# Up-projection of a gated ConvFFN: 28 of 44 pairs of tiles by seven half products in place of eight

## Chip, cores, metric

The kernel runs on one core of a Trainium2 chip. The metric is the device time of one execution in microseconds, the median of several runs; a profiled execution of the same program gives the trace.

## What is computed

Two layers of a hybrid encoder on 768 tokens (512 of one request, 256 of another), all in float32. Each layer has an adaLN norm, one input projection split into dilated window attention and a convolution group, an output projection, and then a gated ConvFFN. The change touches the ConvFFN:

```python
def conv_ffn(h, w_up, dw_w, w_down):
    a, g = jnp.split(h @ w_up, 2, axis=-1)
    g = depthwise_conv(g, dw_w)          # width 3 along the tokens, within each request
    return (a * jax.nn.gelu(g)) @ w_down
# D_MODEL = 1024, D_FF = 2816; in trunk, per layer:
#   h = rms_norm(x, norm2_g[l]) * (1 + s2) + sh2 ;  x = x + g2 * conv_ffn(h, ...)
```

## The kernel before

Activations lie with features on the 128 partitions and the 768 tokens along the free axis. A float32 product is made of three fast ones: every operand is kept as a rounded high part and the remainder, the low part (`hi`, `lo`), and `three` (L349) issues low weight times high activation, high times low, high times high into one PSUM bank. A weight tile is 128 x 1024 (eight slices of 128 x 128, one "unit"). `product` (L358) runs one unit against the eight activation tiles `h`, first the 512 tokens, then the 256: 24 matmuls of 512 columns and 24 of 256.

The 2816 hidden features make 22 pairs of tiles a layer, 44 in all: unit `a` and unit `g` of the up-projection. A pair is two calls of `product`; then `hidden` (L859) scales `g` on ScalarE, adds the two neighbours on VectorE, applies GELU on ScalarE, multiplies by `a` on VectorE, splits the result into `hh` (ScalarE) and `hl` (GpSimd). Pairs come in chunks of 4, 4, 4, 4, 2, 4 (`CHUNKS`). Behind the first pair of a chunk stands `part` (L448), the down-projection of the chunk before, with `nk` units of 48 matmuls each; its results are added to `x` by `accumulate` on VectorE. The last chunk runs its four pairs first, then the part, then `last_part`.

Weights come as a stream of tiles (`stream`, L183). `load_ahead` issues the load of a tile into one of five buffers `raw`; `consume` (L306) splits a tile: `hi` and the negative of the tile on ScalarE (`wh`, `wl`), and a DMA from GpSimd's queue that adds the raw tile to `wl`. Four pairs of `hi`/`lo` buffers (`PAIRS`) hold split units; `unit` pops one, `release` gives it back. In the FFN of layer 0, 56 tiles of the adaLN weights are mixed into the stream (`spread`, `ADA_FFN`); each takes two dot products on VectorE (`ada_dots`, L288).

The order of instructions on each engine is made by the Python program itself: it keeps a clock that the matmuls advance (`tick`), `feed` consumes the next stream item when enough of that clock has passed and buffers are free, and background generators (`conv_bg`) are stepped at a rate. Each engine then runs its own instructions in that order.

Of the kernel before, what the change touches and what calls it, by code (L numbers as in the profile page):

```python
# [15 lines left out]
ALU = mybir.AluOpType  # L16
# [22 lines left out]
ACT = 28  # L39
# [3 lines left out]
ADA_FFN = (2, 56)  # L43
# [13 lines left out]
def encoder(ctx: ExitStack, tc: tile.TileContext, xT, cT, rel_bias, onehot, nlog, wada, wadaT, wada_g2, bada,  # L57
# [19 lines left out]
    def wide(name, w):  # L77
        return act.tile([P, w], F32, tag="wide", name=name, bufs=5)
# [146 lines left out]
    raws = [it[1] if it[0] == "w" else wada[it[3] + KD * (it[2] == 2), it[4]] if it[0] == "a" else wada_g2[it[2] - 40] if it[1] == 0 else wadaT[it[1] - 1, it[2]] for it in stream]  # L225
    loaded = []
    state = {"item": 0, "live": 0, "n": 0, "fed": 0.0, "hold": True}
    ready = []

    def load_ahead(n):  # L230
        while len(loaded) < min(len(raws), n):
            r = wraw.tile([P, 8 * P], F32, tag="raw", name=f"raw{len(loaded)}")
            nc.sync.dma_start(r, raws[len(loaded)])
            loaded.append(r)

# [70 lines left out]
    def consume():  # L306
        i = state["item"]
        it = stream[i]
        state["item"] += 1
        load_ahead(i + RAW)  # L310
        r = loaded[i]
        state["fed"] = clock[0]
        if it[0] == "a":
            ada(*it[1:], r)
            return
        if it[0] == "d":
            ada_dots(*it[1:], r)
            return
        n = state["n"]
        state["n"] += 1  # L320
        state["live"] += 1
        hi = whl.tile([P, 8 * P], F32R, tag="hi", name=f"wh{n}")
        lo = whl.tile([P, 8 * P], F32R, tag="lo", name=f"wl{n}")
# [6 lines left out]
        ready.append((hi, lo))  # L330
# [525 lines left out]
    def ffn(l, K, hs, nxt):  # L856
# [16 lines left out]

        f = 0
        pend = []
        for n, nk in enumerate(CHUNKS):
            hold = nk if n == len(CHUNKS) - 1 else 1
            hid = []
            for i in range(nk):
                if f == 0:  # L880
                    us = [kslices(unit()) for _ in range(2)]
                    a, g = product(us, hs, f"u{l}_{f}", key)
                    release(2)
                else:
                    (a,) = product([kslices(unit())], hs, f"a{l}_{f}")
                    release()
                    (g,) = product([kslices(unit())], hs, f"g{l}_{f}")
                    release()
                hid.append(hidden(f, a, g))
# [28 lines left out]
    load_ahead(RAW)  # L918
# [138 lines left out]
```

## Time and profile before

| | |
|---|---|
| median of 3 runs | 1902.55 us (1900.71 to 1903.45) |
| profiled execution: device time, span | 1892.81 us, 1891.0 us |
| TensorE (PE) busy | 1840.4 us, 97% of the span |
| VectorE (DVE) busy | 1000.3 us, 53% |
| ScalarE (ACT) busy | 816.8 us, 43% |
| GpSimd (POOL) busy | 367.4 us, 19% |
| DMA | 261.81 MB, mean 138 GB/s |

Matmuls are pipelined and their ends are modelled, so the duration of one (0.39 us for 512 columns) is longer than the distance between the starts of two; rates are read from starts. The span is that of the profiled execution; the sums of the prediction are made against it.

### The profile page before, as it was taken

The page shows a single profiled execution, that of the slowest core. Times are in us where ns is not written, and L with a number is a line of the kernel's source. Part 1 is how long each engine was busy: PE and PEld are TensorE (multiplying, and loading weights), DVE is VectorE, ACT ScalarE, POOL GpSimd, SP SyncE. Part 2 cuts the span into 40 slices and gives each one's busy share as a digit, 9 for nine tenths or more (in the row PEclk, how much of TensorE's full clock was granted, in tenths as well). Part 3 has the DMA queues.
Part 4 walks back from the last instruction along what each step waited for, and adds up shares of the span by engine and source line. Part 5 has one row for each costly group of instructions (what it writes and reads, how often), then busy time and mean ns, then how long its engine had stood idle before and what let it go on. Part 6 is the DMA issues. An engine that isn't in the chain of part 4 may idle for free.

```text
span 1891.0 us, 27649 instructions
## 1 busy us (share of the span) xinstructions
PE 1840.4 (97%) x11164; PEld 1552.1 (82%) x11164; DVE 1000.3 (53%) x1779; ACT 816.8 (43%) x1315; POOL 367.4 (19%) x344
## 2 busy tenths in 40 slices
PE   6999999999999999999999999999899999999999
PEld 4789676778888888888878986768788888888888
DVE  6667666776655655664367886666622221313123
ACT  3324667554423242433343357675543333333331
POOL 1103110033211121211232131100521121211110
PEclk9999999999999999999999999999999999999999
DMA  9666431236667777685635542223457464646454
GB/s 339 176 174 192 122 90 44 67 90 162 184 191 199 212 183 212 156 228 147 145 86 127 124 119 64 65 59 97 93 131 162 106 148 112 149 100 151 101 122 112
DMA packets 80913, 261.81 MB, mean 138 GB/s; under 512 B 9137, under 2 KB 18609, under 8 KB 80785
## 3 DMA queue, kind: packets, MB, share of 16 engines
q0 software_dynamic: 26640, 97.01, 28.4%
q1 hardware_dynamic: 54144, 163.03, 25.4%
q8 instruction: 88, 1.44, 0.3%
q14 instruction: 41, 0.33, 0.1%
HBM read 159.83 MB, written 3.18 MB: 86 GB/s over the span
## 4 chain that ended last, share of the span: by engine, by line
PE 90%; DVE 3%; ACT 2%; issue 2%; DMA 2%; POOL 1%; SPq 0%; POOLq 0%; ACTq 0%; DVEq 0%
PE a L351 6%; PE g L351 6%; PE g L352 6%; PE a L352 6%; PE a L350 6%; PE g L350 6%; PE pd L351 5%; PE pd L352 5%; PE pd L350 5%; PE s L729 4%; PE tp L763 2%; PE o L774 2%; PE v L350 1%; DMA wl<-raw 1%; PE q L350 1%
## 5 line engine op out<-in xcount | busy, mean ns | idle before, releaser
L329 POOL DMA_DIRECT2D wl<-raw x185 | 163.9, 886 | 691.1 <-ACT wl L328 498.0
L324 ACT ACTIVATE wh<-raw 128x1024 fp32r<-128x1024 f32 x188 | 197.2, 1049 | 163.4 <-PE pd L352 69.1
L866 DVE SCALAR_TENSOR_TENSOR gc<-g,fw_sb,gc 128x511 f32<-128x511 f32 x84 | 51.4, 612 | 389.6 <-ACT gc L865 389.6
L558 DVE SCALAR_TENSOR_TENSOR acc<-up,cw_sb,acc 128x783 f32<-128x783 f32 x240 | 246.8, 1028 | 4.3
L328 ACT ACTIVATE wl<-raw 128x1024 fp32r<-128x1024 f32 x185 | 193.4, 1046 | 0.0
L351 PE MATMUL pd<-hl,wh 128*128 128x512 f32 (+1 forms) x576 | 193.2, 335 | 0.0
L352 PE MATMUL pd<-hh,wh 128*128 128x512 f32 (+1 forms) x576 | 192.8, 335 | 0.0
L350 PE MATMUL pd<-hh,wl 128*128 128x512 f32 (+1 forms) x576 | 192.4, 334 | 0.0
L871 POOL TENSOR_TENSOR hl<-gc,hh 128x768 fp32r<-128x768 f32 x44 | 81.8, 1860 | 543.5 <-ACT hh L870 543.5
L865 ACT ACTIVATE gc<-g,fw_sb 128x512 f32<-128x512 f32 x84 | 48.2, 573 | 305.6 <-PE g L352 305.6
L292 DVE CUSTOM_DVE_ANT_0 cro<-raw,cr 128x1024 f32<-128x1024 f32 x112 | 166.6, 1488 | 4.2 <-ACT cr L285 1.5
L445 DVE SCALAR_TENSOR_TENSOR x<-pd,mod,x 128x512 f32<-128x512 f32 (+1 forms) x160 | 96.3, 615 | 133.9 <-PE pd L352 133.9
L350 PEld LDWEIGHTS pd<-hh,wl 128*128 128x128 f32 x576 | 108.1, 188 | 12.3
L351 PEld LDWEIGHTS pd<-hl,wh 128*128 128x128 f32 x576 | 108.3, 188 | 11.7
L352 PEld LDWEIGHTS pd<-hh,wh 128*128 128x128 f32 x576 | 108.2, 188 | 11.4
L868 ACT ACTIVATE gc<-gc 128x512 f32<-128x512 f32 x88 | 46.2, 525 | 130.1 <-DVE gc L867 130.1
L729 PE MATMUL s<-kT,qT 64*128 64x512 f32 (+1 forms) x192 | 94.1, 570 | 0.0
L869 DVE TENSOR_TENSOR gc<-a,gc 128x512 f32<-128x512 f32 x84 | 46.9, 558 | 55.0 <-ACT gc L868 55.0
L741 ACT ACTIVATE sp<-sp,nm 128x512 f32<-128x512 f32 (+1 forms) x96 | 62.1, 647 | 27.5 <-DVE nm L739 24.6
L739 DVE CUSTOM_DVE_ANT_0 sp<-s,G 128x512 f32<-128x512 f32 (+1 forms) x96 | 57.1, 596 | 24.0 <-PE s L729 24.0
L750 ACT ACTIVATE sp<-sp,den 128x512 f32<-128x512 f32 (+1 forms) x96 | 61.8, 645 | 9.0 <-DVE den L748 8.8
L764 ACT ACTIVATE PT<-tp 128x512 f32<-128x512 f32 (+1 forms) x96 | 49.3, 518 | 22.5 <-PE tp L763 21.9
(697 smaller groups left out, 5165.2 us busy)
## 6 DMA issues: line engine op xcount, KB each, us to landing
wl<-raw POOLq DMA_DIRECT2D x185, 512.0 KB, 5.8
raw<-in_w_up SPq DMA_DIRECT2D x88, 512.0 KB, 4.7
raw<-in_wadaT SPq DMA_DIRECT2D x48, 512.0 KB, 5.7
raw<-in_w_down SPq DMA_DIRECT2D x44, 512.0 KB, 4.5
raw<-in_w_in SPq DMA_DIRECT2D x40, 512.0 KB, 4.7
raw<-in_wada SPq DMA_DIRECT2D x24, 512.0 KB, 7.0
raw<-in_w_out SPq DMA_DIRECT2D x16, 512.0 KB, 4.7
G<-bt SPq DMA_DIRECT2D x16, 448.0 KB, 4.5
```

The lines of the kernel that those rows point to most:

```text
L292: nc.vector.tensor_tensor_reduce(out=rows["out"], in0=r, in1=rows[g], op0=ALU.mult, op1=ALU.add, scale=1.0, scalar=0.0, accum_out=mod[l][: ...
L324: nc.scalar.activation(hi, r, AF.Copy)
L328: nc.scalar.activation(lo, r, AF.Copy, scale=-1.0)
L329: nc.gpsimd.dma_start(out=lo, in_=r, accum_op=ALU.add)
L350: nc.tensor.matmul(ps, wl, xh, start=first, stop=False)
L351: nc.tensor.matmul(ps, wh, xl, start=False, stop=False)
L352: nc.tensor.matmul(ps, wh, xh, start=False, stop=last)
L445: nc.vector.scalar_tensor_tensor(x[ot][:, span(g)], ps, mod[l][:, gate + ot, g:g + 1], x[ot][:, span(g)], op0=ALU.mult, op1=ALU.add)
L558: nc.vector.scalar_tensor_tensor(a, up[i][:, t:t + ACW], K["cw"][:, l, i, t:t + 1], a, op0=ALU.mult, op1=ALU.add)
L729: nc.tensor.matmul(ps[:, :w], qT[hp][64 * s:64 * s + 64, o + i * P:o + (i + 1) * P], kT[hp][64 * s:64 * s + 64, o:o + w], start=True, stop ...
L741: nc.scalar.activation(sp[:, :w], sp[:, :w], AF.Exp, scale=-1.0, bias=nm, accum_out=den)
L871: nc.gpsimd.tensor_tensor(lo, gc, hi.bitcast(F32), op=ALU.subtract)
```

## The change

In layer 0 the 10 pairs from chunk 3 on, in layer 1 the 18 pairs from chunk 1 on (`SEVEN = (3, 1)`), are computed by Strassen's scheme in the variant with 15 additions. The tokens are cut into two halves of 384 (`HALF`), the 1024 input features into two halves of four tiles, and the two outputs are `a` and `g`: a 2 x 2 product of blocks with seven block products, each of 4 x 3 matmuls of 384 columns (84 in a pair; before 96, of 512 and 256).

- **Weights.** The stream has for such a pair the items A (unit of `a`, split as before), G (the raw tile of `g`, kept), S, B, R. S, B and R make sums of blocks of the raw tiles and split them: sums and low parts on VectorE, high parts on ScalarE. All three are split units in the same four buffers; R overwrites the raw `g` tile.
- **Tokens.** `token_sums` makes 12 split blocks of 384 columns once a layer, as a background generator (`SUMS_FROM`, `SUMS_RATE`), and `last_sums` four more, in place of half of the tiles `h`, just before the first seven-product pair.
- **Products.** `seven(f)` uses three PSUM banks X, Y, Z: X takes the first product, is copied by ScalarE, and goes on accumulating; it is copied twice more. VectorE adds Y and Z to the copies; then convolution, GELU and multiplication as before, from SBUF.
- **The rest of the stream.** The adaLN tiles of layer 0 now lie between items 1 and 29 of the FFN (`ADA_FFN`; before 2 and 56); `token_sums` makes its last four blocks only when none of them is left in the stream. `ACT` grows from 28 to 29 buffers.

```diff
-ACT = 28
+ACT = 29
+HALF = NT // 2
+SEVEN = (3, 1)
+SUMS_FROM = (8, 1)
+SUMS_RATE = (0.7, 1.1)
-ADA_FFN = (2, 56)
+ADA_FFN = (1, 29)
...
+                    ff += [("A", ups[0]), ("G", ups[1]), ("S", None), ("B", None), ("R", None)]
...
+    def split(hi, lo, r):
+        nc.scalar.activation(hi, r, AF.Copy)
+        nc.vector.tensor_tensor(lo, r, hi.bitcast(F32), op=ALU.subtract)
+
+    def sums(n, r, hi, lo):
+        a, g = held["a"], held["g"]
+        s = held["s"] = wraw.tile([P, 8 * P], F32, tag="raw", name=f"sum{n}")
+        nc.vector.tensor_tensor(s[:, :512], g[:, :512], g[:, 512:], op=ALU.add)
+        nc.vector.tensor_tensor(s[:, 512:], s[:, :512], a[:, :512], op=ALU.subtract)
+        split(hi, lo, s)
+
+    def last_block(n, r, hi, lo):
+        split(hi[:, :512], lo[:, :512], held["g"][:, 512:])
+
+    def differences(n, r, hi, lo):
+        a, g, s = held["a"], held["g"], held["s"]
+        nc.vector.tensor_tensor(g[:, :512], a[:, :512], g[:, :512], op=ALU.subtract)
+        nc.vector.tensor_tensor(g[:, 512:], a[:, 512:], s[:, 512:], op=ALU.subtract)
+        split(hi, lo, g)
...
-            if stream[state["item"]][0] != "w" or len(ready) < 2 and state["live"] < PAIRS:
+            kind = stream[state["item"]][0]
+            if kind in "adG" or state["live"] < PAIRS and len(ready) < (2 if kind == "w" else 3):
                 consume()
...
+        def last_sums():
+            for k in range(4):
+                t, u = (tmp(f"{c}4{l}{k}", False)[:, :HALF] for c in "tu")
+                p, q, to = column(k + 4, 0), blocks[1, k], column(k, 1)
+                nc.vector.tensor_tensor(t, p[0].bitcast(F32), q[0].bitcast(F32), op=ALU.subtract)
+                nc.vector.tensor_tensor(u, p[1].bitcast(F32), q[1].bitcast(F32), op=ALU.subtract)
+                nc.vector.tensor_tensor(t, t, u, op=ALU.add)
+                nc.scalar.activation(to[0], t, AF.Copy)
+                nc.vector.tensor_tensor(to[1], t, to[0].bitcast(F32), op=ALU.subtract)
...
+        def seven(f):
...
+            add(X, ua, 0, b11, True)
+            av = af(f"av{tag}")
+            S.activation(av[:, left], X, AF.Copy)
+            add(Y, ua, 1, b21, True)
+            release()
+            V.tensor_tensor(av[:, left], Y, av[:, left], op=ALU.add)
+            us = unit()
+            add(X, us, 1, t2, False)
+            S.activation(av[:, right], X, AF.Copy)
+            add(Z, us, 0, t1, True)
+            release()
+            ub = unit()
+            ur = unit()
+            add(X, ur, 0, t3, False)
+            gv = af(f"gv{tag}")
+            S.activation(gv[:, left], X, AF.Copy)
+            V.tensor_tensor(gv[:, right], Z, gv[:, left], op=ALU.add)
+            add(Y, ub, 0, t4, True)
+            release()
+            V.tensor_tensor(gv[:, left], Y, gv[:, left], op=ALU.add)
+            add(Z, ur, 1, b22, False)
+            release()
+            V.tensor_tensor(av[:, right], Z, av[:, right], op=ALU.add)
...
+                S.activation(z, gv[:, o:o + w], AF.Copy, scale=w1)
+                V.scalar_tensor_tensor(z[:, 1:], gv[:, o:o + w - 1], w0, z[:, 1:], op0=ALU.mult, op1=ALU.add)
+                V.scalar_tensor_tensor(z[:, :w - 1], gv[:, o + 1:o + w], w2, z[:, :w - 1], op0=ALU.mult, op1=ALU.add)
+                S.activation(z, z, AF.Gelu_apprx_tanh)
+            for z, (o, w) in zip(zs, GROUPS):
+                V.tensor_tensor(av[:, o:o + w], av[:, o:o + w], z, op=ALU.mult)
+            hi, lo = at(f"hh{tag}"), at(f"hl{tag}")
+            S.activation(hi, av, AF.Copy)
+            nc.gpsimd.tensor_tensor(lo, av, hi.bitcast(F32), op=ALU.subtract)
...
+            if n == SEVEN[l]:
+                while conv_bg["gen"] is not None:
+                    conv_step(True)
+                last_sums()
             for i in range(nk):
-                if f == 0:
+                if f == SUMS_FROM[l]:
+                    conv_bg.update(gen=token_sums(), rate=SUMS_RATE[l], acc=0.0)
+                if n >= SEVEN[l]:
+                    hid.append(seven(f))
```

Three places in the order of the engines. First ScalarE in layer 1 around the end of pair 5. In the rows a name is tile, layer, pair: `g1_5` is the product g of layer 1, pair 5; `wh`/`wl` are split weights, `hh` the high part of the hidden tile. Before:

```order
L865 ACTIVATE gc1_5_13440<-g1_5_00_13383,fw_sb_265 128x512
L868 ACTIVATE gc1_5_13440<-gc1_5_13440 128x512
L865 ACTIVATE gc1_5_13440<-g1_5_01_13415,fw_sb_265 128x256
L868 ACTIVATE gc1_5_13440<-gc1_5_13440 128x256
L870 ACTIVATE hh1_5_13441<-gc1_5_13440 128x768
L324 ACTIVATE wh140_13461<-raw220_13204 128x1024
L328 ACTIVATE wl140_13462<-raw220_13204 128x1024
```

The change, same place (`gz` is the convolved gate, `wh165` the high part of R for pair 6, the next; `av1_6<-x1_6` the first copy out of bank X of pair 6; `wh166` the unit A of pair 7):

```order
L1053 ACTIVATE gz1_50_13781<-gz1_50_13781 128x512
L1050 ACTIVATE gz1_51_13786<-gv1_5_13748,fw_sb_267 128x256
L1053 ACTIVATE gz1_51_13786<-gz1_51_13786 128x256
L1057 ACTIVATE hh1_5_13793<-av1_5_13684 128x768
L372 ACTIVATE wh165_13803<-raw255_13477 128x1024
L1024 ACTIVATE av1_6_13822<-x1_6_13797 128x384
L360 ACTIVATE wh166_13840<-raw259_13671 128x1024
```

Before, nothing behind the hidden chain of a pair in this queue was read out of PSUM until the next pair's g; now the copy out of bank X of pair 6 stands behind the whole hidden chain of pair 5 and behind the split of R.

VectorE at the same place of the change (`z1_5` is bank Z of pair 5, `raw254`/`raw255` the raw tiles a and g of pair 6):

```order
L1044 TENSOR_TENSOR av1_5_13684<-z1_5_13661,av1_5_13684 128x384
L1051 SCALAR_TENSOR_TENSOR gz1_50_13781<-gv1_5_13748,fw_sb_267,gz1_50_13781 128x511
L1052 SCALAR_TENSOR_TENSOR gz1_50_13781<-gv1_5_13748,fw_sb_267,gz1_50_13781 128x511
L1051 SCALAR_TENSOR_TENSOR gz1_51_13786<-gv1_5_13748,fw_sb_267,gz1_51_13786 128x255
L1052 SCALAR_TENSOR_TENSOR gz1_51_13786<-gv1_5_13748,fw_sb_267,gz1_51_13786 128x255
L1055 TENSOR_TENSOR av1_5_13684<-av1_5_13684,gz1_50_13781 128x512
L1055 TENSOR_TENSOR av1_5_13684<-av1_5_13684,gz1_51_13786 128x256
L391 TENSOR_TENSOR raw255_13477<-raw254_13414,raw255_13477 128x512
L392 TENSOR_TENSOR raw255_13477<-raw254_13414,sum163_13734 128x512
L373 TENSOR_TENSOR wl165_13804<-raw255_13477,wh165_13803 128x1024
```

The two sums of R for pair 6 stand behind the last operation of pair 5, and that chain begins with the last product of pair 5 (bank Z).

Last, ScalarE in layer 1 where the first seven-product pair (pair 4) begins:

```order
L934 ACTIVATE hh1_3_13227<-gc1_3_13226 128x768
L1000 ACTIVATE h11_0h_12442<-t410_13241 128x384
L1000 ACTIVATE h11_1h_12458<-t411_13248 128x384
L1000 ACTIVATE h11_2h_12483<-t412_13255 128x384
L1000 ACTIVATE h11_3h_12504<-t413_13262 128x384
L372 ACTIVATE wh153_13275<-raw241_12849 128x1024
L1024 ACTIVATE av1_4_13294<-x1_4_13269 128x384
```

The four copies of `last_sums` and the split of R stand ahead of the first copy out of bank X of pair 4. Layer 0 has the same rows at pair 12.

## Rows read from the trace of the kernel before

**Rows 1.** The page: busy time of the engines; shares of the chain that ended last.
```profile
PE 1840.4 (97%) x11164; PEld 1552.1 (82%) x11164; DVE 1000.3 (53%) x1779; ACT 816.8 (43%) x1315; POOL 367.4 (19%) x344
...
PE 90%; DVE 3%; ACT 2%; issue 2%; DMA 2%; POOL 1%; SPq 0%; POOLq 0%; ACTq 0%; DVEq 0%
```

**Rows 2.** Windows, the two FFN stages: length, engines' busy us (instructions), PEclk, DMA share, GB/s.
```profile
412.00:950.00 538.00, 531.73 (x3039) 468.02 (x3038) 309.15 (x482) 198.88 (x260) 111.83 (x101) 0.99 0.69 181
...
1335.00:1850.00 515.00, 508.87 (x2952) 447.58 (x2953) 137.01 (x238) 194.19 (x252) 109.96 (x99) 0.99 0.54 125
```

**Rows 3.** Timeline of PE, one product g: start us, us, engine, line, operation.
```profile
501.14 0.39 PE L350 MATMUL g<-h_0h,wl 128*128 128x512 f32 x1
...
506.64 0.28 PE L350 MATMUL g<-h_0h,wl 128*128 128x256 f32 x1
...
509.46 0.39 PE L350 MATMUL pd<-hh,wl 128*128 128x512 f32 x1
```

**Rows 4.** Timeline of DVE in layer 1, one `hidden`; in brackets idle before and its releaser.
```profile
1721.26 0.75 DVE L866 SCALAR_TENSOR_TENSOR gc<-g,fw_sb,gc 128x511 f32<-128x511 f32 x1 [11.56 <-ACT gc L865]
1722.05 0.75 DVE L867 SCALAR_TENSOR_TENSOR gc<-g,fw_sb,gc 128x511 f32<-128x511 f32 x1
1723.56 0.69 DVE L869 TENSOR_TENSOR gc<-a,gc 128x512 f32<-128x512 f32 x1 [0.76 <-ACT gc L868]
1724.17 0.47 DVE L866 SCALAR_TENSOR_TENSOR gc<-g,fw_sb,gc 128x255 f32<-128x255 f32 x1
1724.68 0.48 DVE L867 SCALAR_TENSOR_TENSOR gc<-g,fw_sb,gc 128x255 f32<-128x255 f32 x1
1725.70 0.42 DVE L869 TENSOR_TENSOR gc<-a,gc 128x256 f32<-128x256 f32 x1 [0.54 <-ACT gc L868]
```

**Rows 5.** Timeline of ACT over the same stretch.
```profile
1722.89 0.63 ACT L868 ACTIVATE gc<-gc 128x512 f32<-128x512 f32 x1 [1.67 <-DVE gc L867]
1723.43 0.46 ACT L865 ACTIVATE gc<-g,fw_sb 128x256 f32<-128x256 f32 x1
1725.25 0.42 ACT L868 ACTIVATE gc<-gc 128x256 f32<-128x256 f32 x1 [1.36 <-DVE gc L867]
1726.22 0.85 ACT L870 ACTIVATE hh<-gc 128x768 fp32r<-128x768 f32 x1 [0.55 <-DVE gc L869]
```

**Rows 6.** Groups by line and shape on ACT: busy us, mean ns, idle before and releasers.
```profile
L324 ACT ACTIVATE wh<-raw 128x1024 fp32r<-128x1024 f32 x188 | 197.2, 1049 | 163.4 <-PE pd L352 69.1 <-issue 56.1 <-DMA raw<-in_w_up 38.2
...
L662 ACT ACTIVATE v<-v 128x256 f32<-128x256 f32 x24 | 7.9, 382 | 23.8 <-PE v L352 23.7
...
L678 ACT ACTIVATE hq<-k 128x512 f32<-128x512 f32 x12 | 7.1, 595 | 13.6 <-PE k L352 13.6
```

**Rows 7.** The same groups on DVE.
```profile
L593 DVE TENSOR_TENSOR ls<-ls,ls 128x512 f32<-128x512 f32 x6 | 4.1, 682 | 0.0
...
L593 DVE TENSOR_TENSOR ls<-ls,ls 128x256 f32<-128x256 f32 x6 | 2.5, 420 | 2.6 <-ACT ls L591 2.4
```

**Rows 8.** Windows around two idle stretches of PE; columns as in rows 2.
```profile
370.60:374.10 3.50, 0.02 (x1) 0.00 (x0) 3.50 (x9) 2.90 (x5) 0.00 (x0) 1.00 0.48 150
...
375.60:379.00 3.40, 3.40 (x10) 2.29 (x9) 2.80 (x7) 2.52 (x3) 1.18 (x2) 0.50 0.01 2
...
1333.70:1338.10 4.40, 0.09 (x2) 0.05 (x1) 4.33 (x7) 1.57 (x3) 3.25 (x3) 1.00 0.79 188
1338.10:1341.50 3.40, 3.40 (x8) 2.72 (x9) 3.33 (x6) 1.57 (x3) 2.49 (x2) 0.50 0.52 154
```

**Rows 9.** Line 292 on DVE (duration ns min/median/max), and a piece of its timeline.
```profile
L292 DVE CUSTOM_DVE_ANT_0 cro<-raw,cr x112: 1206/1224/2856, 425.7 to 879.7; 128x1024 f32<-128x1024 f32 x112
...
480.32 2.76 DVE L292 CUSTOM_DVE_ANT_0 cro<-raw,cr 128x1024 f32<-128x1024 f32 x1
...
483.12 1.23 DVE L292 CUSTOM_DVE_ANT_0 cro<-raw,cr 128x1024 f32<-128x1024 f32 x1
```

**Rows 10.** Timeline of POOL over the same stretch.
```profile
480.11 1.88 POOL L871 TENSOR_TENSOR hl<-gc,hh 128x768 fp32r<-128x768 f32 x1 [11.66 <-ACT hh L870]
```

More of the change, by code (lines that the diff above doesn't have):

```diff
@@ L308, in consume, with whole @@
         it = stream[i]
+        load_ahead()
         state["item"] += 1
-        load_ahead(i + RAW)
         r = loaded[i]
         state["fed"] = clock[0]
-        if it[0] == "a":
-            ada(*it[1:], r)
+        if it[0] in "ad":
+            (ada if it[0] == "a" else ada_dots)(*it[1:], r)
+        elif it[0] == "G":
+            held["g"] = r
             return
[L316 to L323, printed above, removed]
+        else:
+            n = state["n"]
+            state["n"] += 1
+            state["live"] += 1
+            hi = whl.tile([P, 8 * P], F32R, tag="hi", name=f"wh{n}")
+            lo = whl.tile([P, 8 * P], F32R, tag="lo", name=f"wl{n}")
+            {"w": whole, "A": first_block, "S": sums, "B": last_block, "R": differences}[it[0]](n, r, hi, lo)
+            ready.append((hi, lo))
+            if it[0] in "AS":
+                return
+            if it[0] == "B":
+                return
+            if it[0] == "R":
+                state["raws"] -= 2
+        state["raws"] -= 1
+        load_ahead()
+    def whole(n, r, hi, lo):
         nc.scalar.activation(hi, r, AF.Copy)
@@ new lines, in last_sums @@
+        def last_sums():
+            for k in range(4):
+                t, u = (tmp(f"{c}4{l}{k}", False)[:, :HALF] for c in "tu")
+                p, q, to = column(k + 4, 0), blocks[1, k], column(k, 1)
+                nc.vector.tensor_tensor(t, p[0].bitcast(F32), q[0].bitcast(F32), op=ALU.subtract)
+                nc.vector.tensor_tensor(u, p[1].bitcast(F32), q[1].bitcast(F32), op=ALU.subtract)
+                nc.vector.tensor_tensor(t, t, u, op=ALU.add)
+                nc.scalar.activation(to[0], t, AF.Copy)
+                nc.vector.tensor_tensor(to[1], t, to[0].bitcast(F32), op=ALU.subtract)
@@ new lines, in seven, with add @@
+        def seven(f):
+            tag = f"{l}_{f}"
+            def add(ps, u, half, xs, first):
+                for k in range(4):
+                    b = slice((4 * half + k) * P, (4 * half + k + 1) * P)
+                    for m, (p, q) in enumerate(((1, 0), (0, 1), (0, 0))):
+                        nc.tensor.matmul(ps, u[p][:, b], xs[k][q], start=first and k == 0 and m == 0, stop=k == 3 and m == 2,
+                                         skip_group_check=True)
+                    tick(3 * (HALF / 2400 + 0.003))
+            b11, b21, b22 = ([column(k + 4 * i, c) for k in range(4)] for i, c in ((0, 0), (1, 0), (1, 1)))
+            t1, t2, t3 = ([blocks[i, k] for k in range(4)] for i in range(3))
+            t4 = [column(k, 1) for k in range(4)]
+            left, right = slice(0, HALF), slice(HALF, NT)
+            V, S = nc.vector, nc.scalar
+            X, Y, Z = (bank(f"{c}{tag}")[:, :HALF] for c in "xyz")
+            ua = unit()
+            add(X, ua, 0, b11, True)
[21 more added lines that the diff above has]
+            V.tensor_tensor(av[:, right], Z, av[:, right], op=ALU.add)
+            w0, w1, w2 = (K["fw"][:, l, f, t:t + 1] for t in range(3))
+            zs = []
+            for g, (o, w) in enumerate(GROUPS):
+                z = tmp(f"gz{tag}{g}", False)[:, :w]
+                zs.append(z)
+                S.activation(z, gv[:, o:o + w], AF.Copy, scale=w1)
[7 more added lines that the diff above has]
+            nc.gpsimd.tensor_tensor(lo, av, hi.bitcast(F32), op=ALU.subtract)
+            return hi, lo
@@ L917, in encoder @@
     load_first(5)
-    load_ahead(RAW)
+    load_ahead()
     hs = [None] * KD
```

104 lines of the change are left out of this document (84 added, 20 removed).

## The prediction

> **What bounds the kernel now.** I read the page's shares first: TensorE is busy 97% of the span, and the chain that ended last lies on it for 90% [rows 1]. The stage table says the same of the two FFN stages: PE 532 of 538 us and 509 of 515 us, while VectorE is busy 309 us in the first, where the adaLN dots run, and 137 us in the second, ScalarE 199 and 194 us [rows 2]. So columns taken from PE are time, and the other engines seem to have room. But those shares are means; what counts is whether they answer within the time that PE's next products give them. Three views give the prices. PE's starts: 24 matmuls of 512 columns take 5.50 us and 24 of 256 take 2.82 us, 0.229 and 0.1175 us each [rows 3]; a product is 8.32 us and a pair 16.63 us. The timelines of one `hidden` give the chain behind a pair, start to start, with the handovers between engines (about 0.1 us) inside [rows 4, 5]. And the windows around PE's idle stretches show its clock [rows 8].
>
> **The change part by part.**
>
> *PE's work.* A matmul of 384 columns lies half-way between the two measured widths: 0.173 us. 84 of them make 14.55 us, 2.08 us less than a pair takes now. Over 28 pairs: **-58.2 us**, if PE never waits.
>
> *Seven products behind seven products.* The order shows the chain. Bank X of a pair takes its first product, is copied by ScalarE, and only then may accumulate the third; between lie X and Y, 24 matmuls, 4.15 us of cover. The copy stands in ScalarE's queue behind GELU, `hh` and the split of R, and R's sums stand on VectorE behind the last multiplications of the pair before. That chain starts when the pair before ends its last product (bank Z). Step by step:
> - handover 0.1, adding bank Z, 384 columns: a two-input operation takes 0.42 at 256 and 0.68 at 512 [rows 7], so 0.55: 0.65 us;
> - two wide convolution steps and the handover to GELU, 1721.26 to 1722.89 [rows 4, 5]: 1.63;
> - GELU, then the narrow scaling, which is behind it in the queue, and its handover: 0.54 + 0.50 [rows 5]: 1.04;
> - two narrow convolution steps, 0.51 + 0.45 [rows 4]: 0.96;
> - the wide multiplication 0.61, the narrow one 0.40 [rows 4]: 1.01;
> - the two sums of R, 512 columns, 0.65 each from start to start [rows 7]: 1.30;
> - handover and R's high part, 1.05 for 1024 columns [rows 6]: 1.15;
> - the copy out of X: 0.38 at 256, 0.60 at 512 [rows 6], so 0.49, and a handover: 0.55.
>
> Together 8.3 us against 4.15: PE stands for about 4.1 us. Nothing later in the pair is late by this count: the copy after the third product comes 2.1 us ahead of the next use of X, R's low part ends about 9.7 us after the start and is needed at 12.4, and the unit A of the next pair lands about 16 us after it and is needed after 18.7. Behind another seven-product pair stand 7 pairs of layer 0 (14, 15, 16, 18 to 21) and 13 of layer 1 (6, 7, 8, 10, 11, 12, 14, 15, 16, 18 to 21): 20 x 4.1 = **+82 us**. The other six (13 and 17; 5, 9, 13, 17) follow a part: there R's sums wait for the part's last buffer only, the copy is done about 3.5 us after the start, inside the cover of 4.15, and I cost them at nothing. That cover has 0.6 us to spare; if it is gone, each costs what is over.
>
> *The clock.* Both windows after an idle stretch of 3.5 and 4.3 us show PE at half its clock (0.50, 1.2 instead of 2.4 GHz) for 3.4 us [rows 8]. The stalls here are as long, so after each I take 3.4 us at half clock, 1.7 us lost. The shorter stretch is a little below my 4.1; below it this argument has no row. 22 stalls (with the two of the next step): **+37 us**; the bounds are 0, and twice that if a second such period follows.
>
> *The first seven-product pair of a layer* (12 and 4). Ahead of the copy out of X stand the rest of `hidden`, `last_sums` and R. `hidden`'s last multiplication ends 2.9 us after PE's last g product (the wide half begins 2.8 us before that end; 0.8 to the first convolution step, 4.44 and 0.42 [rows 4]). `last_sums` goes to ScalarE and back four times: three operations of 384 columns (about 0.5, 0.5, 0.6), a copy (0.1 + 0.53) and the low part (0.1 + 0.47), 2.7 us, so 10.9. R's sums, split and the copy: 3.0. About 17 us, and some 1 us for `hl`, which POOL works on meanwhile (below). Less 4.15: 13.5 us, twice: **+27 us**.
>
> *The adaLN dots and the token sums in layer 0.* Between the hidden parts of pair 0 and the end of the part behind pair 8, PE has 8 x 16.63 + 8 x 8.32 = 200 us of work. VectorE's queue holds 96 dots there (before 48). At 1.23 us [rows 9] and 0.04 between two that is 122, a slow one per pair (2.76 [rows 9]) +1.5 makes 12, eight `hidden` at 4.8 with their waits 38, 16 pairs of additions to x (0.79 and 0.5, as the convolution steps) 21, 28 token sum operations and their eight waits for ScalarE 19: 212 us. PE, with eight banks, can run ahead of VectorE by a few products only. **+12 us**; bounds 0 (the lag stays within the banks) and 30 (the dots' buffers hold up the weights as well).
>
> *At nothing:* S and B and their splits, which need a buffer that the pair before frees 8.3 and 12.5 us after its start and are used in the next pair; the token sums of layer 1 (44 operations of about 0.5 us in three pairs, 50 us). If VectorE's queue were full there, they would delay `hidden` first. POOL's queue issues 28 DMAs of 512 KB fewer (one per pair instead of two, none for S, B, R).
>
> Sum: -58 + 82 + 37 + 27 + 12 = **+100 us**. The profiled execution takes 1892.81 us (span 1891.0); its sum is 1993. The median of the runs is 9.7 us above that execution, so the runs should show **2003 us**.
>
> **The rivals.**
>
> 1. *The stalls don't happen: the saved columns are time.* For it: PE's share, and VectorE at 53% [rows 1]. It decides at 4.15 us from the last product to the copy out of X. If the chain is covered in the 20 pairs, -58 + 27 + 3 + 12 = -16 us, **1887**; with `last_sums` covered too, about 1857. Against it: the convolution, GELU and R's two sums alone are over 6 us. 8%.
> 2. *The stalls come, but the clock stays at 2.4 GHz*: +63 us, **1966**. Against it stand both pairs of windows [rows 8]; for it: the stall is between the two stretches seen, and a chain 10% shorter brings it below both. 16%.
> 3. *GpSimd gets ahead of VectorE.* A dot that starts 0.2 us after POOL's `hl` takes 2.76 us in place of 1.23 [rows 9, 10]. `hl` of the pair before would start about a microsecond after `hh` starts (0.85 us [rows 5] and a handover), some 6.5 us into the chain, while R's second sum starts at about 6.0. If it comes first, the sum waits for 1.88 us and the chain grows by 2.4 us: 20 x 2.4 = +48 us, **2051**. The Trainium skill, "SBUF — State Buffer", section "Who interferes with whom", says that a VectorE instruction with two SBUF inputs and a GpSimd instruction that reads SBUF exclude each other, and that the one that starts first keeps the port to its end. By that rule the trace agrees: 2.76 us is a wait to the end of `hl` and then a whole dot. It also speaks against this change as such, which adds such operations. The margin is half a microsecond; 12%.
>
> **How the numbers follow.** My forecast has 60%, the rivals 8, 16 and 12%; 4% is for an order of waits that I don't see. The range takes in the forecast's bounds (the dots 0 to 30, the clock once or twice, the chain 10% either way, 16 us) and rival 2, and ends at the start of rival 3: 1940 to 2050. It leaves out rival 1 and part of rival 3. A measurement of this kernel can tell 0.2% (3.8 us) from no change. Faster takes rival 1: 0.08; within 0.2%: 0.02; slower: 0.90.
>
> **What would show it.** Right: in the chain and waits of the profile after, PE waits for ScalarE's copy out of X some 20 times, for 3.5 to 5 us each, and twice for over 10 us; PE's share falls from 97% to about 90%; the granted clock drops behind each; the distance of two consecutive seven-product pairs is near 20 us, of a pair behind a part 14.6 us to the next. The second FFN stage grows from 515 to about 560 us. Wrong: waits of under a microsecond there, pairs of 14.6 us throughout, or a stall whose releaser is VectorE's addition or a weight's DMA instead of the copy.

## The result, and the profile after

The changed kernel takes 2018.53 us (2016.37 to 2027.96, 4 runs) against 1901.63 us before (1891.69 to 1903.45, 4 runs beside it): a ratio of 1.0636, 95% interval 1.0585 to 1.0686. The forecast was 2003 us in a range of 1940 to 2050, slower with 0.90. The profiled execution took 2020.33 us, 127.5 more than that of before: it lies 1.8 us above the median of its runs, that of before 9 us below its own.

The page after, busy shares and the chain that ended last:

```profile
PE 1838.8 (91%) x10828; PEld 1594.9 (79%) x10828; DVE 1270.4 (63%) x2207; ACT 893.8 (44%) x1459; POOL 343.5 (17%) x316
...
PE 65%; DVE 18%; ACT 6%; DMA 5%; issue 5%; POOL 1%; SPq 0%; ACTq 0%; DVEq 0%; POOLq 0%
```

TensorE's busy time is the same 1840 us as in [rows 1] although it has 53 us less to do: what the seven products took away came back as work at half the clock, and 6 points of its share became waiting. What it waits for, by the view of waits of the same run (columns: us in total, times, longest):

```profile
PE x L1011 <- ACT av L1024: 109.4, 22, 19.6
```

L1011 is a product of `seven`, L1024 the first copy out of bank X. 22 waits: 20 of 3.79 us, and two at the first seven-product pair of a layer (TensorE's timeline after, the wait in brackets):

```profile
729.89 0.69 PE L1011 MATMUL x<-ts,wl 128*128 128x384 f32 x1 [13.83 <-ACT av L1024]
...
1494.94 0.69 PE L1011 MATMUL x<-ts,wl 128*128 128x384 f32 x1 [19.63 <-ACT av L1024]
```

Windows of the stages after (from the first product of an FFN's start to the next stage; columns as in [rows 2]), then of before with the same borders:

```profile
413.30:1034.60 621.30, 557.63 (x3070) 504.54 (x3069) 418.25 (x679) 240.43 (x335) 110.13 (x96) 0.94 0.55 150
...
1392.70:2018.60 625.90, 546.68 (x2955) 511.48 (x2955) 328.66 (x519) 244.10 (x343) 96.08 (x83) 0.93 0.38 96
```

Before:

```profile
413.30:977.80 564.50, 557.92 (x3203) 491.48 (x3202) 325.67 (x510) 211.33 (x279) 118.20 (x107) 0.99 0.67 175
...
1333.80:1891.00 557.20, 546.36 (x3171) 480.45 (x3171) 151.44 (x261) 196.82 (x255) 111.02 (x101) 0.99 0.53 125
```

The first FFN stage grew by 56.8 us and the second by 68.7; the stage between them took 358.1 us after and 356.0 before. The chain of one stall after, between pairs 6 and 7 of layer 1, in the timelines; VectorE:

```profile
1576.18 0.56 DVE L1044 TENSOR_TENSOR av<-z,av 128x384 f32<-128x384 f32 x1 [0.72 <-PE z L1011]
...
1580.26 1.05 DVE L1055 TENSOR_TENSOR av<-av,gz 128x512 f32<-128x512 f32 x2
1581.23 0.68 DVE L391 TENSOR_TENSOR raw<-raw,raw 128x512 f32<-128x512 f32 x1
1581.83 0.68 DVE L392 TENSOR_TENSOR raw<-raw,sum 128x512 f32<-128x512 f32 x1
1583.70 1.57 DVE L373 TENSOR_TENSOR wl<-raw,wh 128x1024 fp32r<-128x1024 f32 x1 [1.18 <-ACT wh L372]
```

ScalarE in the same stretch:

```profile
1581.34 0.84 ACT L1057 ACTIVATE hh<-av 128x768 fp32r<-128x768 f32 x1 [0.49 <-DVE av L1055]
1582.61 1.06 ACT L372 ACTIVATE wh<-raw 128x1024 fp32r<-128x1024 f32 x1 [0.42 <-DVE raw L392]
1583.57 0.47 ACT L1024 ACTIVATE av<-x 128x384 f32<-128x384 f32 x1
```

And TensorE at its end:

```profile
1584.10 0.69 PE L1011 MATMUL x<-ts,wl 128*128 128x384 f32 x1 [3.79 <-ACT av L1024]
```

Bank Z is done a little before 1576.18; its addition, convolution, GELU and multiplications run to 1581.2, R's sums to 1582.5, R's high part to 1583.6, and the copy that TensorE has needed since 1580.30 comes after them. Pairs 6, 7 and 8 begin here in TensorE's timeline, 20.20 and 20.90 us apart:

```profile
1555.78 0.34 PE L1011 MATMUL x<-h_0h,wl 128*128 128x384 f32 x1
...
1575.98 0.34 PE L1011 MATMUL x<-h_0h,wl 128*128 128x384 f32 x1
...
1596.88 0.34 PE L1011 MATMUL x<-h_0h,wl 128*128 128x384 f32 x1
```

Windows of the run after over pairs 6 and 7 (columns as in [rows 2]), cut where the granted clock falls and rises again:

```profile
1565.20:1568.60 3.40, 3.40 (x13) 3.40 (x12) 1.63 (x3) 1.03 (x2) 0.89 (x1) 0.50 0.74 230
...
1582.30:1589.00 6.70, 4.91 (x15) 4.91 (x16) 3.54 (x5) 3.82 (x5) 2.77 (x2) 0.50 0.66 196
```

With each of the 20 stalls the clock falls to 1.2 GHz, in 14 cases for 3.4 us and in 6 for 6.8 us (the second stall of each row of pairs). The short stretches begin 1.1 to 1.5 us after TensorE has gone on; the long ones begin 1.7 to 1.9 us before it does, while it still stands, so that about 5 us of work lie in them.

### The profile page after: what moved, and what is told of

It is laid out like the page before. It is cut to its first block, busy times and chain, and to the rows that moved or that the text cites. A ratio compares the mean times of both kernels' runs of the same rounds, so it can differ in the third digit from the quotient of the medians.

```text
span 2018.6 us, 27662 instructions
## 1 busy us (share of the span) xinstructions
PE 1838.8 (91%) x10828; PEld 1594.9 (79%) x10828; DVE 1270.4 (63%) x2207; ACT 893.8 (44%) x1459; POOL 343.5 (17%) x316
## 4 chain that ended last, share of the span: by engine, by line
PE 65%; DVE 18%; ACT 6%; DMA 5%; issue 5%; POOL 1%; SPq 0%; ACTq 0%; DVEq 0%; POOLq 0%
PE x L1011 8%; PE z L1011 7%; PE pd L415 4%; PE pd L414 4%; PE pd L416 4%; PE s L793 4%; PE y L1011 4%; DVE cro L316 3%; DMA raw<-in_wadaT 2%; PE tp L827 2%; PE o L838 2%; DMA wl<-raw 2%; PE v L414 1%; DVE gz L1052 1%; DVE gz L1051 1%
## 5 line engine op out<-in xcount | busy, mean ns | idle before, releaser
L360 ACT ACTIVATE wh<-raw 128x1024 fp32r<-128x1024 f32 x160 | 167.9, 1050 | 49.5 <-DMA raw<-in_w_up 31.9
L1011 PE MATMUL x<-ts,wl 128*128 128x384 f32 x224 | 87.7, 391 | 109.4 <-ACT av L1024 109.4
L1011 PEld LDWEIGHTS x<-ts,wl 128*128 128x128 f32 x224 | 48.2, 215 | 116.4 <-ACT av L1024 116.4
L1011 PE MATMUL x<-ts,wh 128*128 128x384 f32 x448 | 134.0, 385 | 0.0
L1058 POOL TENSOR_TENSOR hl<-av,hh 128x768 fp32r<-128x768 f32 x28 | 52.5, 1874 | 371.1 <-ACT hh L1057 371.1
L372 ACT ACTIVATE wh<-raw 128x512 fp32r<-128x512 f32 (+1 forms) x56 | 47.3, 845 | 135.3 <-DVE raw L392 68.7
L1011 PEld LDWEIGHTS x<-ts,wh 128*128 128x128 f32 x448 | 96.7, 222 | 0.0
L373 DVE TENSOR_TENSOR wl<-sum,wh 128x1024 fp32r<-128x1024 f32 x28 | 34.8, 1241 | 92.6 <-ACT wh L372 92.6
L373 DVE TENSOR_TENSOR wl<-raw,wh 128x512 fp32r<-128x512 f32 (+1 forms) x56 | 60.6, 1082 | 38.6 <-ACT wh L372 37.1
L1053 ACT ACTIVATE gz<-gz 128x512 f32<-128x512 f32 (+1 forms) x56 | 29.4, 524 | 112.1 <-DVE gz L1052 112.1
```

Of the source, the lines that this page charges most:

```text
L373: nc.vector.tensor_tensor(lo, r, hi.bitcast(F32), op=ALU.subtract)
L1011: nc.tensor.matmul(ps, u[p][:, b], xs[k][q], start=first and k == 0 and m == 0, stop=k == 3 and m == 2, skip_group_check=True)
```

## The experiments

Each is named by its edit, with the short name, e1 to e10, by which the expectations call it. The ratio is that to the kernel before, timed beside the experiment. A "pair behind a pair" is a seven-product pair that follows another; a "pair behind a part" follows a down-projection.

### Only R held back until the copy is queued (e1)

```diff
+            if kind == "R" and state["late"]:
+                return
...
+            state["late"] = True
             add(X, ua, 0, b11, True)
             S.activation(av[:, left], X, AF.Copy)
+            state["late"] = False
```

> Only R's sums and split are held back until the first copy out of bank X is in the queues. If the stall is the chain of engine queues from bank Z to that copy, its R part goes: in the trace after, the copy starts 1.4 us after hh ends and would start right behind hh. So 20 stalls of 3.79 us become 20 of about 2.4 us, and the time 2018.5 - 20 x 1.4 = 1990 us. If TensorE's clock no longer falls behind the shorter stall, another 40 us go (1950 us). Rival, the stall ends with something other than this copy (a weight, a bank): waits of 3.8 us as before and 2018 us. First pairs keep their waits of about 14 and 20 us (R is behind the copy there too: 1 to 3 us less).

1962.97 us (1956.73 to 1967.98), ratio 1.0341 (1.0295 to 1.0388). The 20 stalls are 2.32 us (one of them 2.59), 1.47 less; in its timeline of ScalarE the copy stands right behind `hh`:

```profile
1543.11 0.84 ACT L1061 ACTIVATE hh<-av 128x768 fp32r<-128x768 f32 x1 [0.49 <-DVE av L1059]
1543.86 0.47 ACT L1027 ACTIVATE av<-x 128x384 f32<-128x384 f32 x1
```

The time fell by 55 us, and the shorter waits make 20 x 1.47 + 5.6 (first pairs, 10.9 and 16.9 us) = 35 of them. The rest is clock: behind the 2.32 us stalls it fell in 6 of the 20 cases. By the traces it gives back some 26 us there; some 10 are lost again in layer 1's attention, where this profiled execution is at half clock for 23.9 us from 1161.4 us on and that of the change for 3.4. Windows behind one stall of each kind, columns as in [rows 2]:

```profile
1779.30:1782.60 3.30, 3.30 (x12) 3.30 (x11) 1.59 (x2) 1.82 (x3) 0.04 (x1) 0.50 0.99 375
1760.60:1775.40 14.80, 14.80 (x84) 14.51 (x84) 9.31 (x14) 7.13 (x10) 2.43 (x2) 1.00 0.39 107
```

So R's link is in the chain with its full length, and the clock is a second price on top of it that a stall does not always pay. The pairs give that price: the distance to the next is 17.2 us where the clock stays, which is 14.6 + 2.32 and 0.26 more, and 18.6 to 18.8 where it falls. A stall costs 0.26 us beyond the wait, a half-clock stretch of 3.4 us some 1.5.

### GELU and what follows behind the copy, R behind both (e2)

```diff
+            def rest():
+                for z, (o, w) in zip(zs, GROUPS):
+                    S.activation(z, z, AF.Gelu_apprx_tanh)
+                    V.tensor_tensor(av[:, o:o + w], av[:, o:o + w], z, op=ALU.mult)
...
+            tail.append(rest)
...
             S.activation(av[:, left], X, AF.Copy)
+            finish()
```

> GELU, multiplications and hh/hl of a pair are put behind the first copy out of bank X of the next pair, and R behind those. Theory: the copy starts when the product is done, 2.1 us after bank Z, so the 20 stalls of 3.79 us and the clock's fall behind them (40 us in all in the trace after) go: 2018.5 - 76 - 40 = 1903 us. One thing late next: the second copy out of X now stands behind R's and unit A's splits, by my count done 9.1 us into the pair and needed at 8.3, so 20 waits of up to 0.8 us, +16: 1903 to 1919 us. Rival, ScalarE or VectorE have no room for the work of a pair (14.6 us of TensorE): pairs of 17 us or more, 1950 us or more. Rival, the copy is not what holds TensorE: no change, 2018.

1906.79 us (1903.67 to 1917.19), ratio 1.0052 (1.003 to 1.0075): 112 us less than the change and still 0.5% slower than the kernel before. TensorE's waits in this run:

```profile
PE x L1013 <- ACT av L1027: 26.3, 2, 15.4
...
PE x L1013 <- ACT av L1035: 6.3, 14, 0.5
```

The 20 waits for the first copy are gone; the two first pairs are left. The second copy (L1035) is now late, by 0.5 us instead of the 0.8 expected: it ends at 1519.27 behind R's and A's splits, and pairs behind a pair take 15.3 us. ScalarE's timeline:

```profile
1517.86 1.04 ACT L364 ACTIVATE wl<-raw 128x1024 fp32r<-128x1024 f32 x1
1518.80 0.47 ACT L1035 ACTIVATE av<-x 128x384 f32<-128x384 f32 x1
```

TensorE's, at the third product of bank X:

```profile
1519.32 0.44 PE L1013 MATMUL x<-ts,wl 128*128 128x384 f32 x1 [0.46 <-ACT av L1035]
```

This shows the cause of the 20 stalls: the work is the same, and only the order of the queues differs.

### TensorE kept busy during the wait (e3)

```diff
+        behind = ((), (6, 7, 8, 10, 11, 12))[l] + (14, 15, 16, 18, 19, 20, 21)
...
             add(Y, ua, 1, b21, True)
+            if f in behind:
+                for q in range(22):
+                    nc.tensor.matmul(Z, ua[0][:, :P], b21[q % 4][0], start=True, stop=True, skip_group_check=True)
             release()
```

> After with work added: in the 20 pairs behind a seven-product pair, 22 extra matmuls of 384 columns (3.8 us at full clock) into bank Z before its first product, between the second product and the one that waits for the copy; they are overwritten and add nothing to the result. If the clock falls because TensorE stands, it now stays at 2.4 GHz and the time falls although 440 matmuls are added: 2018.5 less the 40 us that the half-clock stretches cost in these pairs in the trace after, 1978 us. Rival, the fall of the clock has another cause (the work itself, power): no gain, 2018 us or more. The two first pairs keep their waits and half-clock stretches.

1983.47 us (1982.29 to 1984.94), ratio 1.0458 (1.0425 to 1.049): 35 us less than the change with 440 matmuls more. No half-clock stretch is left in the 20 pairs, and in the view of waits the copy holds TensorE at the two first pairs only:

```profile
PE x L1013 <- ACT av L1026: 34.5, 2, 20.7
```

A pair behind a pair now takes 18.65 us (TensorE's timeline of this run):

```profile
1541.78 0.34 PE L1013 MATMUL x<-h_0h,wl 128*128 128x384 f32 x1
...
1560.42 0.34 PE L1013 MATMUL x<-h_0h,wl 128*128 128x384 f32 x1
```

That is also what a stall of 3.79 us costs by itself (14.6 + 3.79 + the 0.26 of e1), so the clock's part of the 20 pairs is 20.20 less 18.65 in 14 cases and 20.91 less 18.65 in 6: 35 us. The 40 expected left out the 0.26. The clock's fall follows TensorE's standing still, not the work.

### The kernel before with the adaLN tiles moved (e4)

```diff
-ADA_FFN = (2, 56)
+ADA_FFN = (1, 29)
```

> The kernel before, with only the adaLN tiles of layer 0 moved to items 1 to 29. Theory: VectorE alone has room for the dots behind the first pairs (193 of 200 us by my count without token sums), so what is left is the start of the stage, where the trace after has six dots ahead of the norm's n011v and two ahead of the first modulated tile: TensorE idle 9.5 us there against 2.5, and the clock half for 13.7 us against 6.8 (3.4 us lost): about +10 us, 1912 us. Rival, the whole of what the trace after loses there and between 579 and 661 us is the dots': +25 us, 1926. Rival, the dots cost nothing and what is lost is the token sums': 1902.

1903.43 us (1899.0 to 1911.82), ratio 1.0041 (1.0016 to 1.0066), 3 to 12 us. In the trace the stage is some 8 us longer, and 5 of them are at its start, as in the changed kernel, where the norm waits behind the dots (TensorE's timeline):

```profile
437.21 0.69 PE L378 MATMUL nb<-ident,n011r 128*128 128x128 f32 x2 [6.88 <-POOL n011r L385]
440.68 0.58 PE L350 MATMUL u<-h_0h,wl 128*128 128x256 f32 x1 [2.79 <-ACT h_0h L438]
```

Before, these two waits are 1.05 and 1.41 us. (The 5 us are counted from the end of the norm's first wait to the first product of pair 1: 405.52 to 448.47 here, 404.91 to 442.90 before.) Of the 10 us of waits that the changed kernel has between 579 and 661 us, 1.9 are here, 1.24 and 0.63 for a weight. The others come with the token sums; those alone were not tried.

### Token sums of layer 1 issued earlier (e10)

```diff
-SUMS_RATE = (0.7, 1.1)
+SUMS_RATE = (0.7, 2.0)
```

> After with the token sums of layer 1 issued faster (rate 2.0 in place of 1.1), so that the last of them stands ahead of pair 2's hidden chain and not of pair 3's. In the trace after, pair 3's chain begins 3.6 us after its product because VectorE works on S, the last token sums and B first, and the first seven-product pair then waits 19.6 us, not the 13.8 of layer 0. If VectorE's queue there is the cause, the wait falls to 14 to 17 us and the rest stays (a few us, below what one look at the time can tell). Rival, S's and B's splits alone or the port that hl holds are the cause: 19 to 20 us as before.

2023.56 us, one run. The wait of pair 4 fell from 19.63 to 15.34 us, and a new one came ahead of it: the hidden chain of pair 2 now stood behind the token sums and the split of a unit behind that chain on ScalarE, and pair 3 waited for the unit's low part (TensorE's timeline).

```profile
1459.87 0.76 PE L414 MATMUL a<-h_0h,wl 128*128 128x512 f32 x1 [5.91 <-DMA wl<-raw]
1499.01 0.69 PE L1011 MATMUL x<-ts,wl 128*128 128x384 f32 x1 [15.34 <-ACT av L1024]
```

The place of the token sums in VectorE's queue makes 4.3 of the 5.8 us between the layers (S's and B's splits stand where they stood); issuing the sums faster only moves the bill.

### The second copy ahead of unit A, `last_sums` behind the copies (e5)

On top of the order of e2: A is held until the second copy is queued, `last_sums` comes behind that copy, and each low part one tile later.

```diff
-                last_sums()
+                late = [last_sums]
...
             S.activation(av[:, right], X, AF.Copy)
+            state["late"] = ""
+            while late:
+                late.pop()()
...
```

> The kernel of e2 with two more moves. Unit A of the next pair is held until the second copy out of X is queued; and last_sums comes behind that copy in the first seven-product pair, its low parts one tile later (in the token sums too), so that VectorE does not stand for ScalarE. Theory: in the trace of e2 a pair behind a pair takes 15.3 us where one behind a part takes 14.6; the 0.46 us wait for the second copy goes, 20 x 0.65 = 13 us. The waits of the two first pairs (10.9 and 15.4 us in the trace of e2) fall to what the sums need beyond 12.5 us of cover, 1 to 4 us each: -20, and 3 for the clock. 1906.8 - 36 = 1871 us (1863 to 1885). Rival, the second copy only hides the next late thing (R's low part, or unit A's DMA, each now within 0.5 us of its use): pairs stay at 15.2 us and the time near 1882. Rival, the first pairs stand as long for the sixth product as they did for the copy: 1890 or more.

1888.80 us (1884.76 to 1898.03), ratio 0.9965 (0.9946 to 0.9983): 0.35% faster than the kernel before, 0.9% faster than e2 by the ratios, but not the 1871 us expected. The waits of the first pairs came down, from 10.9 to 5.3 us in layer 0 and from 15.37 to 5.6 in layer 1, less far than the 1 to 4 us expected. Layer 1 in TensorE's timeline (between the first two rows stands another such wait, of 1.22 us):

```profile
1436.70 0.44 PE L1030 MATMUL y<-h_1l,wh 128*128 128x384 f32 x1 [1.20 <-DVE h_1l L1018]
...
1443.54 0.69 PE L1030 MATMUL z<-h_4h,wl 128*128 128x384 f32 x1 [3.17 <-DVE gv L1063]
```

A pair behind a pair still takes 15.27 us, as the first rival had it: the second copy hid the next late thing, though not one that it named, the addition of bank Z behind S's low part on VectorE (`sum`, L373, then L1063). VectorE's timeline:

```profile
1522.60 1.23 DVE L373 TENSOR_TENSOR wl<-sum,wh 128x1024 fp32r<-128x1024 f32 x1 [1.19 <-ACT wh L372]
1523.74 0.55 DVE L1063 TENSOR_TENSOR gv<-z,gv 128x384 f32<-128x384 f32 x1
```

TensorE's weight load that waits for it:

```profile
1524.34 0.19 PEld L1030 LDWEIGHTS z<-h_4h,wl 128*128 128x128 f32 x1 [0.50 <-DVE gv L1063]
```

### e5 with the adaLN tiles at items 3 to 31 (e6)

```diff
-ADA_FFN = (1, 29)
+ADA_FFN = (3, 31)
```

> e5 with the adaLN tiles of layer 0 at items 3 to 31 of its FFN in place of 1 to 29. Theory: at the start of the stage the norm of the second token group no longer stands behind six dots (6.9 and 2.8 us of TensorE's idle time there and 3.4 us lost to the clock beyond the kernel before): 8 to 10 us less than e5, of which the dots that move later give back up to 5 in pairs 8 to 11. -3 to -10 us against e5. Rival, those dots only move: same as e5.

1896.51 us (1891.52 to 1904.18), ratio 0.9984 (0.9968 to 1.0001). A miss: 3 to 10 us less than e5 were expected, and it takes some 6 us more (the mean of 12 runs each). The start is as before (1.05 and 1.41 us), but with the dots later a weight and the first copy of pair 12 are late, which they are not in e5. TensorE's timeline:

```profile
691.91 0.76 PE L416 MATMUL a<-h_0h,wl 128*128 128x512 f32 x1 [3.39 <-DMA wl<-raw]
718.24 0.45 PE L1030 MATMUL x<-ts,wl 128*128 128x384 f32 x1 [3.89 <-ACT av L1044]
```

### e5 with unit A's low part on VectorE (e7)

```diff
-        whole(n, r, hi, lo)
+        split(hi, lo, r)
```

> e5 with the low part of unit A on VectorE instead of ScalarE and a DMA of GpSimd: 28 more operations of 1.2 us on VectorE, 28 fewer of 1.05 us on ScalarE, 28 fewer DMAs. If unit A's DMA is what is late in e5's consecutive pairs, they come to 14.6 us and e7 is faster by what e5 lacks (up to 10 us). If VectorE has no room left (by the trace of e2 11.7 us of a pair's 14.6 are busy, and it also stands for ScalarE), its additions of Y and Z come late and pairs grow: 0.3 us or more each, 6 us or more slower than e5.

1908.60 us (1907.31 to 1909.43), ratio 1.0052 (1.0032 to 1.0072): some 17 us slower than without, 0.6 us a pair. One more operation of 1.2 us a pair on VectorE turns the wait for bank Z from 8.5 us in 16 cases into 29.4 in 22, by the views of waits of e5 and of this run:

```profile
PE z L1030 <- DVE gv L1063: 8.5, 16, 3.2
...
PE z L1030 <- DVE gv L1063: 29.4, 22, 3.5
```

### The scheme in layer 1 alone (e8)

```diff
-SEVEN = (3, 1)
-SUMS_FROM = (8, 1)
-ADA_FFN = (1, 29)
+SEVEN = (6, 1)
+SUMS_FROM = (99, 1)
+ADA_FFN = (2, 56)
```

> e5 with the scheme in layer 1 only (18 pairs); layer 0 is that of the kernel before, its adaLN tiles at items 2 to 56 again. Theory: in layer 0 what VectorE gets (token sums and dots) costs more than its ten pairs save: from the first product of that FFN to the first of the next stage the trace of e5 takes 576 us, that of the kernel before 565. So 8 to 11 us less than e5: a ratio to the kernel before of about 0.991 (e5: 0.9965), 1878 us. Rival, ten pairs of 15 us instead of 16.4 pay in layer 0 too: slower than e5.

1880.22 us (1874.38 to 1887.76), ratio 0.9916 (0.9883 to 0.995), the lowest of all, though its interval touches that of e5. Layer 0's FFN with the scheme, up to the next stage, a window of e5 (columns as in [rows 2]):

```profile
417.30:993.20 575.90, 544.93 (x3070) 489.76 (x3069) 422.39 (x684) 238.51 (x336) 113.44 (x98) 0.98 0.60 163
```

Without it, the same window of this run:

```profile
417.30:982.50 565.20, 558.38 (x3203) 491.68 (x3203) 326.10 (x511) 211.27 (x279) 118.79 (x107) 0.99 0.67 175
```

TensorE is 13 us less busy with the scheme, and the window is 11 us longer; e5 is 1.5 us behind at its left border, so 9 us are the stage's. VectorE is busy 422 us instead of 326, and half of TensorE's waits in the first window (16 of 32 us) end with it. The run changes three settings together (the pairs, the token sums, the place of the adaLN tiles), so it shows what the three cost in layer 0, not what each does.

### S's low part behind the addition of bank Z (e9)

```diff
+        low = lambda: nc.vector.tensor_tensor(lo, s, hi.bitcast(F32), op=ALU.subtract)
+        if state["window"]:
+            lows_s.append(low)
...
             V.tensor_tensor(gv[:, right], Z, gv[:, left], op=ALU.add)
+            state["window"] = False
+            while lows_s:
+                lows_s.pop()()
```

> e8 with the low part of S put behind the addition of bank Z to the gate's right half on VectorE. In the trace of e5 TensorE stands 0.2 us for that addition before the last product of a pair that has another behind it, and such pairs take 15.27 us against 14.6. If that is the last late thing but R's low part (0.15), they come to about 14.9 us: 9 of 13 pairs x 0.35 = 3 us less than e8 (0.2%). Rival, S's low part is then late for the next pair, or delays the addition of the second half: no gain, or up to 5 us slower.

1885.19 us (1871.08 to 1891.68), ratio 0.9926 (0.9898 to 0.9954): not told apart from e8. In the trace the step does what it should: most pairs behind a pair take 14.82 us (15.27 in e8), which shows that S's low part was the late thing (window of pair 6, columns as in [rows 2]).

```profile
1500.20:1515.00 14.80, 14.80 (x86) 14.54 (x85) 11.25 (x17) 8.55 (x13) 2.82 (x2) 1.00 0.41 107
```

Its profiled execution has a half-clock stretch of 23.9 us in layer 1's attention, as that of e1 has and that of e8 has not. No edit touches that stage, which takes 369.5 us here and 359.0 in e8; the 3 us sought are smaller than this.

## Why the prediction held, point by point

| term | forecast | trace after |
|---|---|---|
| columns of 28 pairs | -58 | -53 |
| 20 stalls | +82 | +81 |
| clock behind 22 stalls | +37 | +41 |
| two first pairs | +27 | +33 |
| dots and token sums, layer 0 | +12 | +20 |
| the rest | 0 | +6 |
| sum | +100 | +128 |

The mechanism is that of the forecast, term by term; the sum is 28 us short. That the median came within 16 us of 2003 is in part luck: the forecast added 9.7 us because the execution of before lay that far below its median, and that of after does not.

*Columns.* A pair behind a part takes 14.60 us, as worked out (14.55). But the 16.63 us of before is layer 0's; in layer 1 the same execution took 16.43 (last section). 10 x 2.03 + 18 x 1.83 = 53.

*The stalls.* 20 of 3.79 us, forecast 4.1; with the 0.26 us that e1 shows beyond the wait, 4.05 each. Place, number and releaser (what ends the wait) are those of the forecast. The chain from Z's addition to the end of the copy is 1576.18 to 1584.04, 7.9 us: multiplications and R's part were 0.3 us cheaper than my rows. e1 and e2 show the chain: taking R's link out takes 1.47 us, taking the tail out too takes the stall. Rival 1 (the copy is in time anyway) falls. The six pairs behind a part cost nothing, as forecast.

*The clock.* It fell with all 20, so rival 2 falls, and the filled wait shows that the standing still is the reason. Consecutive pairs lie 20.20 or 20.91 us apart, 18.65 without the fall: 1.55 or 2.26 us a stall (14 and 6 cases, 35), and the two first pairs lose some 2.9 and 2.7. The term took 3.4 us each time where 6 stretches were 6.8; that second stretch was inside the bounds. What the prediction held in favour of rival 2 was weak: it took the shortest wait with a fall behind it to be 3.5 us, but in the trace of before the clock is also at half for 6.8 us from 433.59 on, with no longer waits just ahead of it than 1.05 and 1.41 us. e1 shows the same at 2.32 us, in 6 of 20 cases.

*The first pairs.* Layer 0 waits 13.83 us (forecast 13.5), layer 1 19.63. There the step that failed is that of "the token sums of layer 1" at nothing: VectorE worked on S, the last token sums and B before `hidden` of pair 3. VectorE's timeline after, the first two rows in layer 0, the others in layer 1:

```profile
709.94 0.75 DVE L930 SCALAR_TENSOR_TENSOR gc<-g,fw_sb,gc 128x511 f32<-128x511 f32 x1 [4.86 <-ACT gc L929]
...
715.78 2.21 DVE L999 TENSOR_TENSOR t<-t,u 128x384 f32<-128x384 f32 x1
...
1471.44 0.55 DVE L965 TENSOR_TENSOR ts<-h_7h,h_3h 128x384 f32<-128x384 f32 x1
...
1474.17 0.69 DVE L373 TENSOR_TENSOR wl<-raw,wh 128x512 fp32r<-128x512 f32 x1
1474.78 0.74 DVE L930 SCALAR_TENSOR_TENSOR gc<-g,fw_sb,gc 128x511 f32<-128x511 f32 x1
...
1480.59 2.20 DVE L999 TENSOR_TENSOR t<-t,u 128x384 f32<-128x384 f32 x1
```

`gc` of pair 3 starts 3.6 us after its product ended (1471.1); in layer 0 `gc` of pair 11 starts 2 us before its product ends (711.9). That is nearly all of the 5.8 us between the two waits. One addition of `last_sums` takes 2.2 us in place of 0.56 in both layers, since POOL's `hl` started 0.01 us ahead of it and holds it up. The prediction named both ("they would delay `hidden` first", "some 1 us for `hl`") and priced the first at zero because the operations fit in three pairs by their sum; they do not fit by their order, where VectorE stands for ScalarE at each high part. e10, with the token sums earlier, shows it: 15.34 us.

*Dots and token sums.* 20 of 56.8 us are left in layer 0 when columns, stalls, clock and first pair are taken off, inside the bounds of 0 to 30. I had put the cost behind pair 0, and the waits from 579 to 661 us (10 us, with three half-clock stretches) are there; some 5, by e4, are at the start, where more dots stand ahead of the norm of the second token group.

*The rest, and a sign.* 3 of the 6 us are the two rates of 256-column matmuls (last section): after, layer 1 has the longer one, before, the shorter. In layer 0 after half of them have the shorter one, so that some 2 us more belong to dots and token sums. The sign that the second FFN stage "grows from 515 to about 560 us" was too small by the forecast's own terms, which give 53 us in layer 1; it grew by 69.

*GpSimd ahead of R (rival 3).* `hl` of pair 6 starts at 1582.28, 0.45 us behind R's second sum, and that sum keeps its 0.68 us; the margin of half a microsecond held, and 2051 us did not come. What `hl` does delay is R's low part, 1.57 us instead of 1.23, which nobody waits for yet. The Trainium skill, "SBUF — State Buffer", section "Who interferes with whom", has the later of two such instructions wait to the end of the earlier; by that rule the trace agrees, here and for the addition of 2.20 us.

*Open.* How the 10 us of waits between 579 and 661 us divide between dots and token sums was not tried. Why the clock falls within one stall and stays low for 6.8 us, and falls only after the next of the same length and stays low for 3.4, no run shows.

## To carry to other kernels

Saved TensorE columns are time only where each product's operands and banks are free when it starts; write down, per reused bank, what must be read out of it, and in which queue that read stands behind what. A cheap read out of PSUM belongs ahead of the long element-wise tail of the work before it, and moving it there, with R's split behind it (112 us here), is worth more than the 53 us of columns. Check an engine's load by the order and its round trips inside one pair, not by its share of a stage: VectorE was busy 63% of the change's span, and yet, with the copies early, the last waits of the pairs ended with it (e5, e7, e9). The best version (e8) leaves the scheme out in layer 0, where VectorE has the dots as well, and is 0.8% faster than the kernel before.

## What the runs showed of the hardware

A matmul of 256 columns has two rates. In the execution of before, a product's 24 such matmuls take 2.82 us in layer 0 [rows 3] and 2.72 in layer 1, all 42 products of a layer alike; those of 512 columns take 5.50 and 5.49. One product g of layer 1 in TensorE's timeline of before:

```profile
1714.85 0.39 PE L350 MATMUL g<-h_0h,wl 128*128 128x512 f32 x1
...
1720.34 0.28 PE L350 MATMUL g<-h_0h,wl 128*128 128x256 f32 x1
...
1723.06 0.39 PE L350 MATMUL pd<-hh,wl 128*128 128x512 f32 x1
```

In other executions both layers are at the longer figure (e8), or the rate changes within a layer: in that of after, a product of layer 0 takes 8.21 us up to a wait of 1.43 us at 579.60, 8.32 behind it (606.78 to 615.10) and 8.21 again from 670 us on. The clock is granted in full in both. 12 matmuls of 384 columns take 2.08 us in every trace where they don't wait. The Trainium skill, "TensorE: Matmul & The Clock Gate", section "Back-to-back issue gap", has for the gap of a single matmul at full clock the columns by 2.4 GHz and some 2.5 ns; an estimate by it is 109 ns for 256 columns and 162 for 384. The traces have 113 or 118 and 173: they don't agree, and the second rate has no place in it. 42 products at 0.1 us are over 4 us a layer, so a single profiled execution of this kernel is no better than that as a base: a price should be read in the stage, and in the execution, that it is used for. What sets the rate no run shows.
